# Moving gated-attention decay chains between projections, with a stacked low-rank product and an earlier mask load

## The chip, the cores and the metric

One NeuronCore of a Trainium2 chip runs the whole program. The metric is the time of one execution on the device in microseconds (us), from the profiler's first to last instruction plus what lies around it; several executions are timed and the median is given.

## The reference, cut to what matters

The model is a two-layer backbone on 128 context and 1024 latent tokens (1152 columns in all, width 1024). The even layer projects its normalised input `h` with one matrix into queries, keys and values of a windowed attention (`qa`, `ka`, `va`) and of a gated linear attention (`qb`, `kb`, `vb`, `rb`), and into a low-rank input `lr` of 2 x 16 columns, from which the decay of the gated attention comes:

```python
la = log_sigmoid(einsum('btzr,zrk->btzk', lr, w_alpha) + b_alpha) / 16
bcum = cumsum(la over each chunk of 64 tokens)      # forward, and backward for z = 1
q_e, k_e = q * exp(bcum), k * exp(-bcum)
attn = where(tril mask, q_e k_e^T, 0)
```

Queries and keys of the windowed attention are rotated (`rope_2d`) on latent tokens, and the attention reads all context keys beside its window. The odd layer (a gated recurrence) and the two SwiGLU mixers are not touched by the change.

## The kernel before

The kernel works on transposed activations: features on the 128 partitions, 1152 tokens along the free axis, in three chunks of 384. To keep float32 accuracy, an operand is split into a rounded part `hi` (type float32r) and a rest `lo`, and a product is three matmuls, hi*hi, hi*lo, lo*hi (`mm3`, lines 147 to 150). A projection (`proj`, line 300) is 3 chunks x 8 feature blocks x 3 matmuls = 72 matmuls into a PSUM tile named `mm`; there are three of these (line 105). Small products use tiles named `S`, of which there are two (line 111).

Large buffers are numbered slots of 1152 columns, `us(i)`; each slot has one buffer (`bufs=1`), and a later tile of the same number takes it over. Slots 0 and 1, and 32 and 33, are halves of a double buffer made by `up`. Small staging buffers `tmpa` (name `ta`) exist three times. The program is traced in the order of the text; a planner then orders each engine's instructions by program order and by when it expects operands and buffers to be ready, so work that stands later in the text can run earlier where an earlier piece waits. On each engine the order it has chosen is fixed.

The stages around the change are:

- The normalised input H is made chunk by chunk (`norm`, `norm_k`, lines 263 to 287). Chunk 0 is made ahead; chunks 1 and 2 stand in the block loop at blocks 2 and 5. The input X lies in slots 16 to 23 and is overwritten in place (X[5] is slot 21, X[6] slot 22). A norm sums squares (ACT, DVE), reduces over partitions with small matmuls into an `S` tile (lines 229 and 239, copied at line 260), multiplies on POOL (line 267) and shifts and scales on ACT and DVE (lines 272 to 278), through one `S` tile per feature block.
- The block loop (lines 605 to 623) makes, for each of nine blocks of 128 tokens, the token-major values and the low-rank input in two halves of 24 matmuls each (lines 615 to 617). Line 620 copies a half to a `ta` buffer and line 623 copies the 32 low-rank columns from the second half's PSUM tile to `lrs3`.
- Lines 625 to 639 transpose `lrs3` to `lrt` (32 partitions), build the reset mask RM and load the weights `walp`.
- `gla_pre(hd)` (lines 641 to 655), for each of four heads, is the decay chain: three float32 products (line 647), a bias copy on ACT into slot 31 (line 648), exp and log with a table load each (650, 651), two elementwise steps (649, 652), two scans on DVE (653, 654) and a store of slot 30 to `d_b`. All four heads share slots 30 and 31. All four calls stand ahead of the projections in the text.
- Then come the projections of the attention's keys (w_ef[4]), values (w_ef[5]) and four query pairs (w_ef[0] to [3], lines 677 to 724), with `rope` on DVE and POOL, key stacks on ACT and DVE (`kstack`, lines 711 and 713) and stores to `d_qa`, which `attention` (lines 733 to 832) reads back for all four pairs at once.
- `gla_init` (line 854) stands behind the last attention block; it loads the masks `gmask` through a `ta` buffer. `gla_a` loads the initial states (`sgla`) through another `ta` buffer (lines 904 to 906), and `gla_b` runs the state scans (942, 943).

Of the kernel before, what the change touches and what calls it, by code (L numbers as in the profile page):

```python
# [8 lines left out]
F32R = mybir.dt.float32r  # L9
# [3 lines left out]
ALU = mybir.AluOpType  # L13
# [5 lines left out]
CW = 384  # L19
# [4 lines left out]
U = T  # L24
# [22 lines left out]
def body(tc, A):  # L47
    nc = tc.nc
    ve, sc, pe, gp, sy = nc.vector, nc.scalar, nc.tensor, nc.gpsimd, nc.sync

    def f_(ap):
        return ap.bitcast(F32)

    with contextlib.ExitStack() as ctx:
# [16 lines left out]
        mq = st.tile([128, 2, 128], U8, name="mq")  # L71
        m2 = st.tile([128, 128], F32, name="m2")
# [6 lines left out]
        def up(i, dt=F32):  # L79

            pair[i] = pu.tile([128, 2 * U], dt, tag=f"u{i}", name=f"u{i}", bufs=1)
            return pair[i]

        def us(i, dt=F32):

            if i in (0, 32):
                return up(i, dt)[:, :U]
            if i in (1, 33):
                return pair[i - 1][:, U:]
            return pu.tile([128, U], dt, tag=f"u{i}", name=f"u{i}", bufs=1)  # L90
# [7 lines left out]
        def mmps():  # L98
            if wide[0]:
                wide[0] = wide[0] % 8 + 1  # L100
                if wide[0] > 3 and wide[0] <= wide[1]:
                    return aux(*(("X", 2), ("X", 2), ("S", 2), ("S", 2), ("O", 1))[wide[0] - 4])
                if wide[0] > wide[1]:
                    wide[0] = 1
            return pm.tile([128, 512], F32, name="mm", bufs=3)

        def tmpa(n=CW):
            t = pt.tile([128, CW], F32, name="ta", bufs=3)
            return t[:, :n]

        def aux(tag="S", bufs=2):
            return pm.tile([128, 512], F32, name=tag, bufs=bufs)
# [8 lines left out]
        def wtile():  # L121

            if wext:
                wpos[0] = (wpos[0] + 1) % (4 + len(wext))
                if wpos[0] >= 4:
                    i = wext[wpos[0] - 4]
                    return uc(i - 100, F32R) if i >= 100 else us(i, F32R)[:, :D]
            return pw.tile([128, D], F32R, name="w", bufs=4)
# [3 lines left out]
        def wload(ap, n=D, slots=None, he=None):  # L132
            raw = pw.tile([128, D], F32, name="raw", bufs=3)
            sy.dma_start(out=raw[:, :n], in_=ap)
            if slots:
                hi, lo = us(slots[0], F32R), us(slots[1], F32R)
            else:
                hi, lo = wtile(), wtile()
            (he or wcopy[0])(hi[:, :n], raw[:, :n])  # L139
            gp.tensor_tensor(out=lo[:, :n], in0=raw[:, :n], in1=f_(hi[:, :n]), op=ALU.subtract)  # L140
            return hi, lo

        def split(hi, lo, src, e=None):
            sc.copy(hi, src)
            return (e or ve).tensor_tensor(out=lo, in0=src, in1=f_(hi), op=ALU.subtract)  # L145
# [13 lines left out]
        def ch(c):  # L159
            return slice(c * CW, (c + 1) * CW)  # L160
# [11 lines left out]
        def load_x(c):  # L172
            for k in range(8):
                sy.dma_start(out=X[k][:, ch(c)], in_=A["xT"][k, :, ch(c)])
# [117 lines left out]
        def projc(w, H, evict, c):  # L292
            hi, lo = w
            ps = mmps()
            for k in range(8):
                s = slice(k * 128, (k + 1) * 128)
                mm3(ps[:, :CW], hi[:, s], lo[:, s], H[0][k][:, ch(c)], H[1][k][:, ch(c)], k == 0, k == 7)
            evict(c, ps[:, :CW])

        def proj(w, H, evict):  # L300
            for c in range(NCH):
                projc(w, H, evict, c)
# [259 lines left out]
        d_qa = dr.tile([4, 128, T], F32, name="d_qa")  # L562
# [22 lines left out]
        H = [[None] * 8, [None] * 8]  # L585
# [15 lines left out]
                    sc.copy(wh[:, s], raw)  # L601
                    (gp if hf == 0 or i else ve).tensor_tensor(out=wl[:, s], in0=raw, in1=f_(wh[:, s]), op=ALU.subtract)
        load_x(2)
        lrs3 = us(32)[:, :288].rearrange("p (b n) -> p b n", b=9)
        for blk in range(9):
            if blk in (2, 5):
                norm(0, 0, X, H, 1 if blk == 2 else 2, inplace=True)
# [1 line left out]
            for hf in range(2):  # L609
                ps = mmps()  # L610
# [7 lines left out]
                n = 272 if hf == 0 else 240  # L618
# [3 lines left out]
                if hf == 1:  # L622
                    ve.tensor_copy(lrs3[:, blk], ps[:, 240:272])

        lrt = us(33)[0:32]
        for b0, b1 in ((0, 4), (4, 8), (8, 9)):
            ps = aux()
            n = (b1 - b0) * 128
            for b in range(b0, b1):
                pe.transpose(ps[0:32, (b - b0) * 128:(b - b0 + 1) * 128], lrs3[:, b], ident)  # L630
            ve.tensor_copy(lrt[:, b0 * 128:b1 * 128], ps[0:32, :n])

        RM = us(23)
        gp.memset(RM, 1.0)
        rm = RM.rearrange("p (c t) -> p c t", t=64)
        gp.memset(rm[0:64, :, 0:1], 0.0)
        gp.memset(rm[64:128, :, 63:64], 0.0)
        walp = us(22)[0:32, :512].rearrange("p (h n) -> p h n", h=4)
        sy.dma_start(out=walp, in_=A["w_alp"])

        def gla_pre(hd):

            et, bt = us(31), us(30)
            bal = cols[:, C_BALPHA + hd:C_BALPHA + hd + 1]
            for c in range(NCH):
                ps = aux()
                pe.matmul(ps[:, :CW], walp[:, hd], lrt[:, ch(c)], start=True, stop=True)
                sc.activation(out=et[:, ch(c)], in_=ps[:, :CW], func=AF.Identity, bias=bal)
            ve.scalar_tensor_tensor(bt, et, -1.0, et, op0=ALU.mult, op1=ALU.min)
            sc.activation(out=bt, in_=bt, func=AF.Exp)  # L650
            sc.activation(out=bt, in_=bt, func=AF.Ln, bias=1.0)
            ve.scalar_tensor_tensor(et, et, 0.0, bt, op0=ALU.min, op1=ALU.subtract)
            ve.tensor_tensor_scan(bt[0:64], RM[0:64], et[0:64], 0.0, op0=ALU.mult, op1=ALU.add)
            ve.tensor_tensor_scan(bt[64:128, ::-1], RM[64:128, ::-1], et[64:128, ::-1], 0.0, op0=ALU.mult, op1=ALU.add)
            sy.dma_start(out=d_b[hd], in_=bt)

        for hd in range(4):
            gla_pre(hd)

        COS, SIN = us(16), us(17)  # L660
        sy.dma_start(out=COS[:, :TL], in_=A["rope"][0])
        sy.dma_start(out=SIN[:, :TL], in_=A["rope"][1])
# [1 line left out]
        def rope(t):  # L664
            x = t[:, TC:T]
            r = us(19)[:, :TL]
            ve.stream_shuffle(r, x, [(i + 16) % 32 for i in range(32)])
            ve.tensor_tensor(out=x, in0=x, in1=COS[:, :TL], op=ALU.mult)
            gp.tensor_tensor(out=r, in0=r, in1=SIN[:, :TL], op=ALU.mult)
            ve.tensor_tensor(out=x, in0=x, in1=r, op=ALU.add)  # L670

        def ev_to(t):
            def ev(c, ps):
                sc.copy(t[:, ch(c)], ps)
            return ev

        KA, VST = us(18), us(20)
        proj(wload(A["w_ef"][4]), H, ev_to(KA))
        sy.dma_start(out=A["o_ck"], in_=KA[:, :TC])
        rope(KA)  # L680
        proj(wload(A["w_ef"][5]), H, ev_to(VST))
# [1 line left out]

        KK = [[us(24 + g * 2 + part, F32R) for part in range(2)] for g in range(2)]
        VA = [us(28, F32R), us(29, F32R)]
        SM = us(30, F32R)
        cst = tmpa(256)
        sy.dma_start(out=cst[:, 0:128], in_=A["cache_v"])
        sy.dma_start(out=cst[:, 128:256], in_=A["cache_k"])
        split(SM[:, 0:128], SM[:, 128:256], cst[:, 0:128])  # L690

        def va(part, blk):
            if blk == 9:
                return SM[:, part * 128:part * 128 + 128]
            return VA[part][:, blk * 128:(blk + 1) * 128]

        def kkc(g, part):
            o = 256 + (g * 2 + part) * 128
            return SM[:, o:o + 128]

        for b0, b1 in ((0, 4), (4, 8), (8, 9)):
            ps = aux()
            n = (b1 - b0) * 128
            for b in range(b0, b1):
                pe.transpose(ps[:, (b - b0) * 128:(b - b0 + 1) * 128], VST[:, b * 128:(b + 1) * 128], ident)
            split(VA[0][:, b0 * 128:b1 * 128], VA[1][:, b0 * 128:b1 * 128], ps[:, :n])

# [9 lines left out]
            kstack(cst[:, 128:256], KK[g][0][:, TL:U], KK[g][1][:, TL:U], g)  # L717
            kstack(KA[:, 0:TC], kkc(g, 0), kkc(g, 1), g)

        for j in range(4):  # L720
            q = us(21 + j % 2)
            proj(wload(A["w_ef"][j]), H, ev_to(q))
            rope(q)
            sy.dma_start(out=d_qa[j], in_=q)

# [126 lines left out]
        atr = [0]  # L852

        def gla_init():
            mqf = tmpa(384)
            sy.dma_start(out=mqf, in_=A["gmask"])
            ve.tensor_copy(mq.rearrange("p a b -> p (a b)"), mqf[:, :256])
            ve.tensor_copy(m2, mqf[:, 256:])
            t = us(12)
            gp.memset(t[:, :1024], 0.0)  # L860
            G["AT"] = [t[:, :512], t[:, 512:1024]]
# [144 lines left out]
        for i in range(9):  # L1006
            attention(i - 1)
            if i < 8:
                proj(wload(A["w_ef"][6 + i]), H, ev_spill(d_qk[i], 0.125 if i < 2 else 1.0) if i < 4 else ev_spill(d_r[i - 4], None))
            ada_step(2)  # L1010
            if i == 8:
                gla_init()
                gla_a(0)
# [242 lines left out]
        for blk in range(3):  # L1256
# [3 lines left out]
            g = gates_a(blk, 1)  # L1260
# [172 lines left out]
```

## Time and profile before

| what | value |
|---|---|
| median of 3 runs | 2864.69 us (2863.2 to 2864.82) |
| profiled execution | 2866.14 us, span 2864.4 us |
| PE busy (matmul) | 2671.9 us, 93% of the span |
| DVE, ACT, POOL busy | 71%, 47%, 45% |
| mean granted TensorE clock | 0.96 of full speed |
| chain that ended last | PE 73%, DVE 12%, ACT 5%, DMA 5% |

PE is the TensorE, PEld its weight loads, DVE the VectorE, ACT the ScalarE, POOL the GpSimd, SP the engine that issues most transfers. Busy PE time can hide small gaps, because matmuls overlap. The granted clock says which share of 2.4 GHz the TensorE ran at; 0.50 is the 1.2 GHz level.

### The profile page before, as it was taken

The numbers are of one execution on the slowest core, as the hardware profiler recorded it, in microseconds if no ns is written. First come the engines' busy times: TensorE is split into PE (matmuls) and PEld (weight loads), VectorE is DVE, ScalarE is ACT, GpSimd is POOL, SyncE is SP. The second block draws the span as 40 slices with busy tenths as digits, with TensorE's granted clock in tenths as the row PEclk, the third lists the DMA queues.
The fourth block names the chain that finished last, engine by engine and source line by source line (L and its number), as shares of the span: only waits on it lengthen the run. The fifth ranks groups of instructions, "written<-read, shape, count | busy, mean of one in ns | idle before, by whom it ended". The sixth has DMA issues, their size and how long they took to land.

```text
span 2864.4 us, 48327 instructions
## 1 busy us (share of the span) xinstructions
PE 2671.9 (93%) x18588; PEld 2540.8 (89%) x18588; DVE 2036.7 (71%) x3536; ACT 1333.5 (47%) x2402; POOL 1280.0 (45%) x767
## 2 busy tenths in 40 slices
PE   6999996888899999999999989896899999999998
PEld 4888884556899999999999989896899999999998
DVE  5466677653688877778786566657788777788876
ACT  5445556434543434444335567563543533444333
POOL 4231014223555556455556433333555555455453
PEclk8999997889999999999999999898999999999999
DMA  7125347643342233523223133373342233433322
GB/s 280 58 94 170 127 151 235 198 138 123 109 174 87 84 101 101 202 85 101 82 86 121 61 104 101 110 238 131 129 158 82 89 96 119 162 92 107 101 82 71
DMA packets 136966, 353.64 MB, mean 123 GB/s; under 512 B 14592, under 2 KB 61824, under 8 KB 136736
## 3 DMA queue, kind: packets, MB, share of 16 engines
q1 hardware_dynamic: 135008, 343.48, 36.3%
q0 software_dynamic: 1728, 7.08, 0.7%
q8 instruction: 146, 2.39, 0.3%
q14 instruction: 84, 0.69, 0.1%
HBM read 286.20 MB, written 64.30 MB: 122 GB/s over the span
## 4 chain that ended last, share of the span: by engine, by line
PE 73%; DVE 12%; ACT 5%; DMA 5%; issue 3%; POOL 1%; SPq 0%; DVEq 0%; ACTq 0%; POOLq 0%
PE mm L150 10%; PE mm L148 10%; PE mm L149 10%; PE X L150 5%; PE X L148 5%; PE X L149 5%; PE S L148 4%; PE S L150 4%; PE S L149 4%; PE O L148 2%; PE O L150 2%; PE O L149 2%; PE mm L192 1%; PE X L814 1%; DVE u L943 1%
## 5 line engine op out<-in xcount | busy, mean ns | idle before, releaser
L150 PE MATMUL mm<-u,w 128*128 128x384 f32 (+1 forms) x1320 | 420.9, 321 | 2.4 <-DVE w L458 2.0
L148 PE MATMUL mm<-u,w 128*128 128x288 f32 (+1 forms) x1234 | 396.6, 322 | 25.0 <-DVE u L317 23.1
L149 PE MATMUL mm<-u,w 128*128 128x288 f32 (+1 forms) x1234 | 393.4, 319 | 3.2 <-POOL u L145 3.2
L140 POOL TENSOR_TENSOR w<-raw,w 128x1024 fp32r<-128x1024 f32 (+1 forms) x66 | 150.3, 2278 | 361.3 <-ACT w L139 306.8
L148 PEld LDWEIGHTS mm<-u,w 128*128 128x128 f32 x1234 | 235.5, 191 | 33.8 <-issue 27.9
L150 PEld LDWEIGHTS mm<-u,w 128*128 128x128 f32 x1320 | 251.0, 190 | 7.5 <-issue 4.3
L149 PEld LDWEIGHTS mm<-u,w 128*128 128x128 f32 x1234 | 235.2, 191 | 4.6 <-POOL u L145 3.4
L150 PE MATMUL mm<-u,u 128*128 128x288 f32 x693 | 204.0, 296 | 0.0
L148 PE MATMUL S<-u,w 128*128 128x288 f32 (+1 forms) x526 | 164.9, 314 | 38.9 <-ACT t L1177 33.5
L317 DVE SCALAR_TENSOR_TENSOR u<-mm,mods,u 128x288 f32<-128x288 f32 (+4 forms) x345 | 145.8, 451 | 74.4 <-PE mm L150 73.7
L150 PE MATMUL X<-u,w 128*128 128x288 f32 (+1 forms) x630 | 192.8, 307 | 1.6 <-DVE w L450 1.6
L148 PE MATMUL mm<-u,u 128*128 128x288 f32 x627 | 186.5, 298 | 4.0 <-ACT u L444 3.8
L149 PE MATMUL mm<-u,u 128*128 128x288 f32 x627 | 185.3, 296 | 0.0
L148 PE MATMUL X<-u,w 128*128 128x288 f32 (+1 forms) x580 | 176.2, 306 | 1.4 <-DVE u L145 1.2
L149 PE MATMUL X<-u,w 128*128 128x288 f32 (+1 forms) x580 | 176.3, 305 | 1.1 <-DVE u L278 1.1
L149 PE MATMUL S<-u,w 128*128 128x288 f32 (+1 forms) x526 | 163.5, 311 | 0.0
L148 PE MATMUL mm<-u,c 128*128 128x288 f32 (+2 forms) x497 | 152.4, 307 | 0.7 <-DVE ta L505 0.7
L451 POOL TENSOR_TENSOR u<-raw 128x512 f32<-128x512 f32 x82 | 136.0, 1658 | 35.2 <-DMA raw<-in_w_fi_dram 19.4
L149 PE MATMUL mm<-u,c 128*128 128x288 f32 (+2 forms) x497 | 151.4, 305 | 0.0
L447 DVE TENSOR_TENSOR u<-u,raw 128x512 f32<-128x512 f32 x82 | 140.3, 1711 | 0.8
L148 PEld LDWEIGHTS S<-u,w 128*128 128x128 f32 x526 | 101.7, 193 | 41.8 <-ACT t L1177 35.6
L148 PE MATMUL X<-u,u 128*128 128x288 f32 (+1 forms) x444 | 131.9, 297 | 2.2 <-DVE u L145 1.5
(443 smaller groups left out, 9114.9 us busy)
## 6 DMA issues: line engine op xcount, KB each, us to landing
raw<-in_w_fi_dram SPq DMA_DIRECT2D x164, 512.0 KB, 3.6
raw<-in_w_fo_dram SPq DMA_DIRECT2D x96, 384.0 KB, 3.1
raw<-in_w_ada_dram SPq DMA_DIRECT2D x48, 512.0 KB, 4.9
c<-in_w_ada_dram SPq DMA_DIRECT2D x32, 512.0 KB, 5.9
d_w<-u SPq DMA_DIRECT2D x20, 512.0 KB, 4.0
u<-d_w SPq DMA_DIRECT2D x20, 512.0 KB, 4.8
u<-in_w_ada_dram SPq DMA_DIRECT2D x16, 512.0 KB, 10.3
raw<-in_w_fo_dram SPq DMA_DIRECT2D x16, 512.0 KB, 3.7
```

Source lines behind the costliest of these rows:

```text
L140: gp.tensor_tensor(out=lo[:, :n], in0=raw[:, :n], in1=f_(hi[:, :n]), op=ALU.subtract)
L148: pe.matmul(ps, wh, hh, start=first, stop=False)
L149: pe.matmul(ps, wh, hl, start=False, stop=False)
L150: pe.matmul(ps, wl, hh, start=False, stop=last)
L192: pe.matmul(ps[32 * g:32 * g + 32, :256], scp[:, 4 * p + g], raw[:, g * 256:(g + 1) * 256], start=p == 0, stop=p == 1)
L317: ve.scalar_tensor_tensor(x, ps[:, s0:s1], mod(l, j, cond, n), x, op0=ALU.mult, op1=ALU.add)
L447: ve.tensor_tensor(out=s2, in0=s1, in1=a11, op=ALU.subtract)
L451: gp.tensor_tensor(out=s3, in0=a11, in1=a21, op=ALU.subtract)
L814: pe.transpose(px[:, i * 128:(i + 1) * 128], P[i][:, kb * 128:(kb + 1) * 128], ident)
L943: ve.tensor_tensor_scan(kv[Bk, ::-1], D0[Bk, ::-1], kv[Bk, ::-1], 0.0, op0=ALU.mult, op1=ALU.add)
```

## The change

`lrs3` moves from slot 32 to slot 21. `lrt` becomes a stack of three 32-row groups (hi, hi, lo) in slot 32 and `walp` a stack (hi, lo, hi) in slot 22, so that one matmul over 96 partitions gives hi*hi + hi*lo + lo*hi; the raw weights are loaded to slot 20. The four `gla_pre` calls are put behind the projections of the keys, of queries 0, of queries 1 and of queries 2. Queries 0 and 1 are projected, rotated and stored before the value transposes and the key stacks, in slots 21 and 28; queries 2 keep slot 21 and queries 3 take slot 22. The mask load of `gla_init` moves ahead of the loads of the rotation tables.

```diff
-        lrs3 = us(32)[:, :288].rearrange("p (b n) -> p b n", b=9)
+        lrs3 = us(21)[:, :288].rearrange("p (b n) -> p b n", b=9)
...
-        lrt = us(33)[0:32]
+        lrt = up(32, F32R)[:, :U]
...
-            ve.tensor_copy(lrt[:, b0 * 128:b1 * 128], ps[0:32, :n])
+            g = slice(b0 * 128, b1 * 128)
+            for q in range(2):
+                sc.copy(lrt[q * 32:q * 32 + 32, g], ps[0:32, :n])
+            ve.tensor_tensor(out=lrt[64:96, g], in0=ps[0:32, :n], in1=f_(lrt[0:32, g]), op=ALU.subtract)
...
-        walp = us(22)[0:32, :512].rearrange("p (h n) -> p h n", h=4)
-        sy.dma_start(out=walp, in_=A["w_alp"])
+        walp = us(22, F32R)[:, :512]
+        wa = us(20)[0:32, :512]
+        sy.dma_start(out=wa.rearrange("p (h n) -> p h n", h=4), in_=A["w_alp"])
+        for q in range(2):
+            sc.copy(walp[q * 64:q * 64 + 32], wa)
+        ve.tensor_tensor(out=walp[32:64], in0=wa, in1=f_(walp[0:32]), op=ALU.subtract)
...
-                pe.matmul(ps[:, :CW], walp[:, hd], lrt[:, ch(c)], start=True, stop=True)
+                pe.matmul(ps[:, :CW], walp[0:96, hd * 128:hd * 128 + 128], lrt[0:96, ch(c)], start=True, stop=True)
...
-        for hd in range(4):
-            gla_pre(hd)
-
+        mqf = tmpa(384)
+        sy.dma_start(out=mqf, in_=A["gmask"])
+        ve.tensor_copy(mq.rearrange("p a b -> p (a b)"), mqf[:, :256])
+        ve.tensor_copy(m2, mqf[:, 256:])
...
-        KA, VST = us(18), us(20)
+        KA = us(18)
         proj(wload(A["w_ef"][4]), H, ev_to(KA))
+        gla_pre(0)
+        VST = us(20)
...
+        for j in range(2):
+            q = us(21 if j == 0 else 28)
+            proj(wload(A["w_ef"][j]), H, ev_to(q))
+            gla_pre(j + 1)
+            rope(q)
+            sy.dma_start(out=d_qa[j], in_=q)
+        q2 = us(21)
+        proj(wload(A["w_ef"][2]), H, ev_to(q2))
+        gla_pre(3)
         SM = us(30, F32R)
...
-        for j in range(4):
-            q = us(21 + j % 2)
-            proj(wload(A["w_ef"][j]), H, ev_to(q))
+        for j in range(2, 4):
+            q = q2
+            if j == 3:
+                q = us(22)
+                proj(wload(A["w_ef"][j]), H, ev_to(q))
             rope(q)
             sy.dma_start(out=d_qa[j], in_=q)
...
         def gla_init():
-            mqf = tmpa(384)
-            sy.dma_start(out=mqf, in_=A["gmask"])
-            ve.tensor_copy(mq.rearrange("p a b -> p (a b)"), mqf[:, :256])
-            ve.tensor_copy(m2, mqf[:, 256:])
```

## Rows read from the trace of the kernel before

**Rows 1.** The page's 40 slices (71.6 us each): busy tenths of PE.
```profile
PE   6999996888899999999999989896899999999998
```

**Rows 2.** Waits, 100 to 230 us: total us, times, longest us.
```profile
PE S L647 <- ACT u L648: 8.5, 3, 6.7
```

**Rows 3.** Stages: us, busy PE PEld DVE ACT POOL, granted clock, DMA share, GB/s.
```profile
109.50:131.10 21.60, 20.85 (x100) 16.72 (x99) 9.95 (x6) 9.03 (x11) 4.40 (x1) 1.00 0.01 4
131.10:149.50 18.40, 17.73 (x90) 15.38 (x90) 12.25 (x11) 13.28 (x16) 4.91 (x2) 1.00 0.20 65
149.50:163.00 13.50, 6.80 (x15) 4.25 (x15) 7.44 (x3) 6.31 (x8) 1.12 (x1) 0.62 0.24 84
...
480.00:500.00 20.00, 6.47 (x45) 6.20 (x45) 17.65 (x12) 8.96 (x20) 17.20 (x10) 0.59 0.33 99
```

**Rows 4.** Lines 623, 639 (ns min/median/max, first/last start) and timeline (start, us).
```profile
L623 DVE COPY u<-mm x9: 173/181/181, 56.2 to 105.5; 128x32 f32<-128x32 f32 x9
...
L639 SPq EVENT_SEMAPHORE  x1: 1452/1452/1452, 87.2 to 87.2; - x1
...
87.50 0.68 ACT L275 ACTIVATE S<-u,mods 128x384 f32<-128x384 f32 x1 [0.57 <-DVE u L278]
87.98 0.68 DVE L273 TENSOR_SCALAR S<-u,mods 128x384 f32<-128x384 f32 x1
```

**Rows 5.** Timeline of PE at the end of block 2.
```profile
67.63 0.39 PE L616 MATMUL mm<-u,u 128*128 128x272 f32 x1 [1.06 <-DVE u L278]
```

**Rows 6.** Timeline: norm of chunk 1, then chunk 2.
```profile
53.47 0.50 PE L229 MATMUL S<-ones,t 128*128 128x1 f32 x4
...
56.52 0.48 ACT L260 COPY t<-S 128x384 f32<-128x384 f32 x1
...
66.33 0.78 DVE L254 TENSOR_TENSOR t<-t 128x384 f32<-128x384 f32 x1
...
72.94 0.56 DVE L278 TENSOR_TENSOR u<-S,u 128x384 fp32r<-128x384 f32 x1 [0.85 <-ACT u L277]
...
80.91 7.84 POOL L267 TENSOR_TENSOR u<-u,t 128x384 f32<-128x384 f32 x8 [11.97 <-ACT t L260]
```

**Rows 7.** Timeline of PE behind the longest wait.
```profile
160.52 0.52 PE L149 MATMUL mm<-u,w 128*128 128x384 f32 x1
160.84 0.52 PE L150 MATMUL mm<-u,w 128*128 128x384 f32 x1
...
163.22 0.34 PE L149 MATMUL mm<-u,w 128*128 128x384 f32 x1
163.39 0.33 PE L150 MATMUL mm<-u,w 128*128 128x384 f32 x1
```

**Rows 8.** Timeline of PE at the first low-rank product.
```profile
109.57 0.91 PE L647 MATMUL S<-u,u 32*128 32x384 f32 x2
...
110.41 0.45 PE L148 MATMUL mm<-u,w 128*128 128x384 f32 x1
```

**Rows 9.** Timeline of the chains: ACT and PE.
```profile
116.28 0.58 ACT L648 ACTIVATE u<-S,cols 128x384 f32<-128x384 f32 x1 [1.16 <-PE S L647]
...
131.14 1.05 ACT L648 ACTIVATE u<-S,cols 128x384 f32<-128x384 f32 x2 [6.61 <-DVE u L654]
...
131.77 0.91 PE L647 MATMUL S<-u,u 32*128 32x384 f32 x2 [1.43 <-ACT u L648]
...
156.26 1.65 PE L647 MATMUL S<-u,u 32*128 32x384 f32 x2 [6.70 <-ACT u L648]
...
175.26 1.05 ACT L648 ACTIVATE u<-S,cols 128x384 f32<-128x384 f32 x2 [9.16 <-DVE u L654]
```

**Rows 10.** Line 858, SP's timeline, and the chain that ended last.
```profile
L858 DVE COPY m<-ta x1: 221/221/221, 477.9 to 477.9; 128x128 f32<-128x128 f32 x1
...
471.04 0.46 SPq L856 DMA_DIRECT2D ta<-in_gmask_dram  x1
...
478.90 2.03 issue
```

## The prediction
> **What bounds the kernel now.** I read the page's slices first, then the waits of TensorE, then its busy time by stage. The slices show PE at nine tenths or more nearly everywhere [rows 1], so a microsecond added to or taken from PE's queue is a microsecond of the kernel unless a later stage has slack. The change acts between 45 and 222 us: the nine value blocks (to 105 us) and the stage of projections and decay chains behind them. In the block stage PE is full, with 1.06 us idle [rows 5]. In the next stage it has two kinds of loss. One is a wait: the low-rank matmuls of line 647 wait 8.5 us for line 648, 6.7 us of that in one wait [rows 2]; line 648 in turn waits for the scan of line 654 before it may overwrite its operand [rows 9]. The other is the clock: 149.5 to 163 us ran at a mean grant of 0.62 of full speed [rows 3]. The attention stage behind it, to about 420 us, shows only nines [rows 1], so whatever the change does up to 222 us is passed on. After it, PE has a hole of 13.5 us at 480 to 500 us [rows 3], where head 0 of the gated part starts; the early masks touch that.
>
> **Part 1: `lrs3` moves from slot 32 to slot 21.** This is the largest term and it is a loss. Slot 21 holds X[5] until the third norm (chunk 2), which stands in the program behind the fifth block. Does a new owner of a slot wait for the last reader of the old one, even where the bytes are already free? The kernel before answers: `walp` takes columns 0 to 511 of slot 22 (X[6]), chunk 2 of X[6] is columns 768 to 1151, and SP still waited 1.45 us until 88.65 us, where a last reading of X[6] on DVE ends (87.98 + 0.68 [rows 4]). So it waits. X[5]'s last reader is line 275 at 87.50 us [rows 4], and the first of the nine line-623 copies into `lrs3` ran at 56.2 us [rows 4]. In the new kernel that copy can't run before X[5] is done, and until then its PSUM bank (one of three named mm) isn't free. Blocks 0, 1 and 2 leave one bank each behind; with all three taken PE can't begin block 3. Queued behind it on PE are all later blocks and the key projection; all of these take mm banks, only the norm's small S matmuls still go.
>
> PE ends block 2 at about 66.2 us, where the row with the 1.06 us wait stands [rows 5]. When does X[5] come free? Its sum of squares ends at 66.33 + 0.78 = 67.1 [rows 6]. From the first matmul of a norm's reduction to the copy of line 260 it took 56.52 - 53.47 = 3.05 us for chunk 1 [rows 6]; then 0.48 for the copy, six of the eight multiplies on POOL (7.84 x 6/8 = 5.9 [rows 6]) and 0.68 for line 275 [rows 4]: 10.1 us, so 77.2 us at the earliest. At the latest the reduction gets one of the two S banks only when the second norm is done at 72.94 + 0.56 = 73.5 [rows 6]: then 83.6. I take the middle, 80.4. Wait: 80.4 - 66.2 = 14.2, less the 1.06 that was there: 13.1 us (bounds 10.0 and 16.3). Then the clock: after the 6.70 us wait at 149.5, groups of line 148 to 150 stepped at 0.32 us (160.52 to 160.84) instead of 0.17 (163.22 to 163.39) until about 162.9 [rows 7], 6.6 us at the 1.2 GHz level, so 3.3 us lost. A longer wait should cost the same once. **Part 1: +16.4 us** (10.0 to 19.6).
>
> **Part 2: float32 products become one stacked product.** Each of the 12 products of line 647 is two instructions and holds PE from 109.57 to the next start at 110.41, 0.84 us [rows 8]; a one-pass matmul of the same 384 columns steps by 0.17 [rows 7]. 12 x (0.84 - 0.17) = **-8.0 us**, on PE's own queue. No row shows a stacked product of 96 partitions; I price it as a row of 128, and from below 0 us saved if it needed the old time. The Trainium skill ("FP8 and Floating Point Precision", TensorE Precision Notes) states that a true float32 product takes four passes. By that the old one costs 4 x 0.17 = 0.68 and the saving is 6.1 us; the row's 0.84 decides, so I keep 8.0.
>
> The splits around it (six ACT copies and three DVE subtractions for `lrt`, two and one for `walp`) lie beside the blocks and the key projection, where ACT has 9.0 of 21.6 us busy and DVE 10.0 [rows 3]: nothing. Without that cover the last group alone would be late by about two 0.6 us copies. `walp` is now loaded through a slot (20) that comes free by the same norm; the first low-rank product is behind 12.5 us of projection (72 matmuls x 0.174), so this wait hides too.
>
> **Part 3: the chains are spread.** A chain is line 648, 649, two table loads with Exp and Ln, 652 and two scans. From one head's last bias copy to the next head's first it took 116.28 to 131.14, 14.9 us, for head 0; from product to product or copy 24.5 us (131.77 to 156.26) and 19.0 (to 175.26) for heads 1 and 2 [rows 9]. Before, the four ran one behind the other from 110 us. Now head 0 starts behind the key projection and head 1 only behind two more projections (25 us, against 15 to 19 for the chain), so that wait goes. Heads 2 and 3 each have one projection (12.5 us of PE) before them and a chain of about 19 us: their third product still waits for the scan of the head before, because the two S banks hold the first two. Which PE work the planner puts ahead of it decides how much is idle. Before, it put 17.8 us of PE work (131.77 to 149.56, where the 6.70 us wait begins) against head 1's chain of 24.5. I expect 4 us at each of heads 2 and 3, 8.5 in all as before, but in shorter pieces, without the drop of the clock: the 1.43 us wait at 131.77 [rows 9] left the grant at 1.00 [rows 3]. **-3.3 us**, bounds -11.8 (8.5 and 3.3 both gone) and 0.
>
> **Part 4: masks early.** The mask load (SP, 471.04) took a `ta` buffer ahead of the states of line 905, and a 2.03 us wait at 478.90 in the chain stands before the copies of lines 921 and 928 that go ahead of head 0's scan [rows 10]; the mask's casts end at 478.1 [rows 10]. With that buffer free the wait goes: **-2.0 us**, bounds 0 (the scan waits for the state's landing anyway) and -4. On SP the early mask passes between the block stores; `ta` has three buffers there and the blocks will be waiting for PSUM: nothing. Moving the stores of queries 0 and 1 earlier gains nothing, since attention needs all four.
>
> **Sum.** 16.4 - 8.0 - 3.3 - 2.0 = +3.1 us on the profiled execution's 2866.14 us: 2869.2. The runs' median stands 1.45 below that execution, so 2867.8; I say 2868. A measurement tells about 0.2% (5.7 us, so 2859 to 2870.4) from no change; the forecast is inside.
>
> **Rivals.**
> *The slot isn't held* (1 in 10): the planner gives `lrs3` its place at once. Against it stands the `walp` row. Then part 1 is 0: -13.3, 2851.
> *The wait is at its short end and spreading works fully* (2 in 10): X[5] free at 77.2 and no low clock after the many small norm matmuls (+10.0), no chain waits (-11.8): 10.0 - 8.0 - 11.8 - 2.0 = -11.8, 2853; halfway to it, 2860. For it: 25 us before head 1, and the key stacks (line 711, four casts in the 24.5 us chain) now fall beside head 0. Against: heads 2 and 3.
> *The bank handover* (1 in 4, the other side): the third norm's reduction gets no S bank until the second norm is finished, because each tile of that norm stands ahead of it. Place: between 67.1 and 73.5 us; price: part 1 at 19.6. It decides if X[5] is free after 82 us. With part 3 at its half, 19.6 - 8.0 - 1.6 - 2.0 = +8.0: 2873; with neither part 3 nor part 4, +11.6: 2876.
> *The forecast* (0.45): own range 2863 to 2873.
>
> Chances from these: faster by over 0.2%: the first rival and most of the second, 0.26; slower: the third less its low end, and the top of the forecast, 0.33; the same 0.41. Range 2853 to 2878: it takes the second rival and the third and leaves the first and the far ends out.
>
> **What would show it.** In the new trace: the first copy into `lrs3` behind the last reading of X[5] at 77 to 84 us; a hole in PE from about 66 us, then 6 us at the low clock; the blocks ending at about 120 instead of 105. The low-rank products as 12 single instructions stepping by 0.17. Two shorter waits for the scan, at heads 2 and 3, none at head 1. The scan of head 0 of the gated part about 2 us nearer to its states. If the copies into `lrs3` run while X[5] is still in use, part 1 is wrong and the kernel is faster; if the blocks end at 105 the whole forecast falls.

## The result, and the profile after

The changed kernel takes 2882.06 us (median of 4 runs, 2879.95 to 2884.67); the kernel before, run beside it, 2864.11 us. The ratio is 1.0061 with a 95% interval of 1.0049 to 1.0073. Against the 2864.69 us that the forecast started from, that is 17.4 us slower, where 3.1 us were forecast; the stated range ended at 2878 us. The profiled execution's span is 2879.7 us, 15.3 more than before, at a mean granted clock of 0.96 as before.

The loss is in the block stage. The copies of line 623, which answer to [rows 4] (ns min/median/max, first/last start):

```profile
L623 DVE COPY u<-mm x9: 179/181/181, 84.3 to 123.1; 128x32 f32<-128x32 f32 x9
```

The first copy moved from 56.2 to 84.3 us and the last, the end of the blocks, from 105.5 to 123.1: 17.6 us. The timeline of PE, ACT, POOL and DVE in the changed kernel shows the hole, in place of the 1.06 us of [rows 5]:

```profile
65.14 0.39 PE L615 MATMUL mm<-u,u 128*128 128x272 f32 x1 [2.79 <-ACT ta L620]
...
68.14 0.29 PE L617 MATMUL mm<-u,u 128*128 128x272 f32 x1
72.68 1.44 PE L229 MATMUL S<-ones,t 128*128 128x1 f32 x6 [4.25 <-DVE u L278]
...
84.62 0.57 PE L615 MATMUL mm<-u,u 128*128 128x272 f32 x1 [8.29 <-DVE u L623]
84.99 0.43 PE L616 MATMUL mm<-u,u 128*128 128x272 f32 x1
...
76.92 7.67 POOL L267 TENSOR_TENSOR u<-u,t 128x384 f32<-128x384 f32 x8 [8.19 <-ACT t L260]
...
83.20 0.68 ACT L275 ACTIVATE S<-u,mods 128x384 f32<-128x384 f32 x1 [0.37 <-DVE u L278]
```

Read it downwards. With blocks 0 and 1 each holding a bank, only one is left for the two halves of block 2: the second half waits 2.79 us for the copy of the first (line 620), a wait that the kernel before does not have there. Block 2 ends at 68.4 us. The third norm's reduction (line 229) waits 4.25 us for line 278, the last step of the second norm for a feature block, and begins at 72.68: it got no `S` bank before. POOL multiplies from 76.92, X[5] has its last reader, line 275, at 83.20 + 0.68 = 83.9, and 0.4 us later the first copy into `lrs3` frees the bank for block 3. The windows give the price (us, busy PE, PEld, DVE, ACT, POOL, granted clock, DMA share, GB/s), first after, then before:

```profile
45.00:66.00 21.00, 17.41 (x128) 16.76 (x127) 16.20 (x25) 15.12 (x31) 14.71 (x10) 0.95 0.56 177
66.00:85.00 19.00, 5.90 (x34) 5.33 (x33) 12.70 (x27) 11.16 (x21) 10.41 (x11) 0.63 0.23 72
85.00:105.00 20.00, 20.00 (x150) 20.00 (x150) 3.23 (x10) 3.45 (x7) 1.30 (x3) 0.93 0.10 35
```
```profile
45.00:66.00 21.00, 21.00 (x151) 21.00 (x150) 16.27 (x27) 15.05 (x32) 14.52 (x10) 0.87 0.59 193
66.00:85.00 19.00, 17.94 (x144) 17.72 (x143) 9.84 (x23) 8.88 (x18) 7.03 (x8) 1.00 0.19 60
85.00:105.00 20.00, 20.00 (x162) 19.90 (x161) 6.48 (x16) 5.74 (x11) 5.06 (x7) 1.00 0.29 94
```

PE is busy 43.3 us of these 60 instead of 58.9, 15.6 us less. The low clock behind the hole is short: some 14 matmuls step by 0.23 us instead of 0.13 until 88.0, about 1.5 us.

What should have come back behind the blocks hardly did. From the blocks' end to the first attention matmul it took 116.9 us before (105.5 to 222.4) and 114.9 after (123.1 to 238.0). The stage in windows, after (columns as above):

```profile
160.00:180.00 20.00, 20.00 (x117) 20.00 (x116) 12.92 (x8) 10.02 (x13) 8.36 (x3) 1.00 0.24 91
180.00:198.00 18.00, 15.29 (x88) 14.90 (x86) 11.88 (x9) 8.60 (x11) 5.60 (x2) 1.00 0.27 96
198.00:211.00 13.00, 7.15 (x36) 6.77 (x35) 10.65 (x8) 4.56 (x8) 3.74 (x2) 0.74 0.30 107
...
226.00:238.00 12.00, 6.46 (x39) 5.16 (x40) 5.75 (x10) 3.75 (x10) 2.37 (x1) 0.72 0.71 246
```

PE is full to 180 us, and then has two holes with a low grant, at 198 to 211 and 226 to 238. Where [rows 3] had one hole of that kind (6.80 of 13.50 us, 0.62), there are now two. The rows that end them, the last query's copy on ACT (line 682), and DVE in front of the second hole; the last row is DVE in the kernel before, where the last query's rotation begins:

```profile
136.02 0.51 PE L654 MATMUL S<-u,u 96*128 96x384 f32 x2
136.36 0.34 PE L148 MATMUL mm<-u,w 128*128 128x384 f32 x1
...
184.40 0.44 PE L654 MATMUL S<-u,u 96*128 96x384 f32 x1 [2.71 <-ACT u L655]
...
204.10 0.69 PE L654 MATMUL S<-u,u 96*128 96x384 f32 x1 [5.85 <-ACT u L655]
...
231.54 1.93 PE L192 MATMUL mm<-c,scp 128*32 128x256 f32 x16 [5.55 <-DVE t L865]
...
203.47 1.05 ACT L655 ACTIVATE u<-S,cols 128x384 f32<-128x384 f32 x2 [7.41 <-DVE u L661]
...
215.91 0.49 ACT L682 COPY u<-mm 128x384 f32<-128x384 f32 x1
```
```profile
216.35 4.39 DVE L660 TENSOR_TENSOR_SCAN u<-u,u 64x1152 f32<-64x1152 f32 x1
220.76 2.55 DVE L661 TENSOR_TENSOR_SCAN u<-u,u 64x1152 f32<-64x1152 f32 x1
...
223.56 1.36 DVE L675 STREAM_SHUFFLE u<-u 128x1024 f32<-128x1024 f32 x1
...
229.05 1.23 DVE L678 TENSOR_TENSOR u<-u,u 128x1024 f32<-128x1024 f32 x1
230.92 0.56 DVE L865 TENSOR_SCALAR t<-mm 128x384 f32<-128x384 f32 x1
```
```profile
208.48 0.01 DVE L667 LOAD_MASK_SELECT u<-u  x1 [0.46 <-ACT u L674]
```

The product (now line 654) steps by 0.17 us as priced (two from 136.02 to 136.36). But it waits 2.71 and 5.85 us at heads 2 and 3, together as much as the 8.5 us of [rows 2], because line 655 still waits for the scan of the head before. And the fourth chain's scans stand on DVE in front of the last query's rotation (223.56) and the copy of line 865 (230.92), for which PE waits another 5.55 us. The query that is rotated there was copied by 216.4 (215.91 + 0.49), so its rotation begins 7.2 us late. Before, that rotation began at 208.5, as soon as the copy was done (line 674), with nothing of a chain in front of it.

### The profile page after: what moved, and what is told of

Read it like the earlier page. It is cut to its first block, busy times and chain, and to the rows that moved or that the text cites. A ratio compares the mean times of both kernels' runs of the same rounds, so it can differ in the third digit from the quotient of the medians.

```text
span 2879.7 us, 48327 instructions
## 1 busy us (share of the span) xinstructions
PE 2662.9 (92%) x18576; PEld 2540.2 (88%) x18576; DVE 2026.5 (70%) x3537; ACT 1335.8 (46%) x2409; POOL 1282.8 (45%) x767
## 4 chain that ended last, share of the span: by engine, by line
PE 72%; DVE 12%; ACT 6%; DMA 5%; issue 4%; POOL 1%; SPq 0%; DVEq 0%; ACTq 0%; POOLq 0%
PE mm L150 10%; PE mm L148 10%; PE mm L149 9%; PE X L148 5%; PE X L150 5%; PE X L149 5%; PE S L148 4%; PE S L150 4%; PE S L149 4%; PE O L148 2%; PE O L150 2%; PE O L149 2%; PE mm L192 1%; DMA raw<-in_w_fi_dram 1%; DMA ta<-d_y 1%
```

## The experiments

A ratio is always to the kernel before, run beside it on the same chip; 0.1% is 2.9 us. Milestones of the profiled executions, in us:

| kernel | blocks' end | last scan starts | last query copied | its rotation starts | first attention matmul | ratio |
|---|---|---|---|---|---|---|
| before | 105.5 | 192.5 | 208.4 | 208.5 | 222.4 | 1 |
| changed | 123.1 | 220.8 | 216.4 | 223.6 | 238.0 | 1.0061 |
| before_same | 105.7 | 192.7 | 208.8 | 208.8 | 222.9 | 0.9987 |
| before_hold | 123.9 | 212.6 | 228.7 | 228.7 | 242.7 | 1.0059 |
| after_nohold | 105.8 | 202.8 | 198.4 | 205.6 | 221.2 | 0.9989 |
| before_order | 106.1 | 203.1 | 203.4 | 205.9 | 221.1 | 1.0008 |
| before_stack | 105.7 | 190.7 | 207.2 | 207.3 | 221.1 | 0.9975 |
| before_stack_again | 105.7 | 190.6 | 206.7 | 206.7 | 220.5 | 0.9969 |
| before_mask | 106.1 | 193.1 | 209.2 | 209.3 | 223.3 | 0.9999 |
| before_two | 106.0 | 168.1 | 210.4 | 210.5 | 224.5 | 1.0003 |
| stack_two | 108.8 | 175.3 | 208.9 | 208.9 | 222.8 | 0.9982 |
| before_two26 | 105.7 | 166.3 | 202.0 | 202.1 | 216.1 | 0.9973 |
| stack_two26 | 106.3 | 173.9 | 203.5 | 203.5 | 217.3 | 0.9960 |
| stack_two26_again | 105.0 | 172.7 | 201.8 | 201.8 | 215.7 | 0.9965 |
| nohold_two26 | 105.8 | 203.6 | 199.1 | 206.2 | 222.5 | 0.9997 |
| nohold_early3 | 106.4 | 195.3 | 205.2 | 208.4 | 222.1 | 0.9986 |

The two columns in the middle show who sets the attention's start. In the old order of chains the last query's rotation starts within 0.1 us of the query's copy, and the attention 13.8 to 14.1 us after that copy, in all eleven profiles. In the new order the copy comes as much as 10.0 us earlier (after_nohold, 198.4 for 208.4), but the rotation starts 2.5 to 7.2 us behind it, because other work stands ahead of it on DVE.

**The scale of the noise: before_same.** The kernel before with no edit.

> The kernel before itself once more, as a measure of what two equal programs show, and for a profile on this chip: ratio 1.000 within 0.0015; attention starts at 222 us and the state scans at 483 us, as in the first profile.

2864.4 us, 0.9987 [0.9977, 0.9997]. The interval leaves out 1 for two equal programs, and the low-rank waits were 5.4 us in this profile and 8.5 in the other. So a difference of 0.13% is nothing here, whatever its interval says, and neither are 3 us of waits in one profile.

**The hold alone: before_hold.** The kernel before with `lrs3` in slot 21; `lrt` keeps the columns of slot 33.

```diff
-        lrs3 = us(32)[:, :288].rearrange("p (b n) -> p b n", b=9)
+        lrs3 = us(21)[:, :288].rearrange("p (b n) -> p b n", b=9)
...
-        lrt = us(33)[0:32]
+        lrt = up(32)[0:32, U:]
```

> The kernel before with one thing done: lrs3 in slot 21. Theory A: the first copy into lrs3 runs at about 84 us, the blocks end at about 123 us, and the time is 2864 plus 13 to 18: 2877 to 2882 us. Rival B: the delay is given back by the waits for the scans (8.5 us before) and the time is 2864 to 2870 us.

2881.38 us, 1.0059 [1.0041, 1.0076], which is 16.9 us (11.8 to 21.8). Waits of PE from 40 to 240 us (total, times, longest):

```profile
PE mm L615 <- DVE u L623: 8.3, 1, 8.3
PE S L647 <- ACT u L648: 6.9, 3, 5.1
...
PE S L229 <- DVE u L278: 2.9, 1, 2.9
PE mm L615 <- ACT ta L620: 2.8, 1, 2.8
```

One slot number costs what the whole change costs, with the same waits at lines 615 and 229 (the second one shorter, 2.9 us).

**All but the hold: after_nohold.** The changed kernel with a buffer of its own for the copies (`small` is cut from 128 to 112 columns to make room).

```diff
-        lrs3 = us(21)[:, :288].rearrange("p (b n) -> p b n", b=9)
+        lrs3 = st.tile([128, 288], F32, name="lrs").rearrange("p (b n) -> p b n", b=9)
```

> The changed kernel with one thing undone: lrs3 gets a buffer of its own instead of slot 21. Theory A (the slot held by X[5] is the loss): the three block tiles come free at once, TensorE's hole between 62 and 85 us is gone, the blocks end at 105 instead of 123 us, and 13 to 18 us of the loss go: 2864 to 2869 us. Rival B (the loss is made later, by the new order of chains and queries or by what the planner makes of the stages behind; the early hole would have been absorbed): blocks end at 105 but the time stays above 2875 us.

2863.48 us, 0.9989 [0.9977, 1.0001]: -3.2 us (-6.6 to +0.3), inside what two equal programs show. The blocks end at 105.8 again. The hold is worth 20.6 us here (1.0061 - 0.9989), a little over the 13 to 18 of theory A. From both sides the hold is the loss; and the rest, priced at -13.3 us, is worth little.

**The order alone: before_order.** The kernel before with the new places of the four chains and of queries 0 and 1.

```diff
-        for hd in range(4):
-            gla_pre(hd)
...
         proj(wload(A["w_ef"][4]), H, ev_to(KA))
+        gla_pre(0)
...
+        for j in range(2):
+            q = us(21 if j == 0 else 28)
+            proj(wload(A["w_ef"][j]), H, ev_to(q))
+            gla_pre(j + 1)
...
+        proj(wload(A["w_ef"][2]), H, ev_to(q2))
+        gla_pre(3)
```

> The kernel before with the new order of chains and queries alone (float32 products, lrs3 in slot 32, masks late). Theory C (the four chains follow each other at about 20 us each wherever they stand, and the last query's rotation stands behind the last scan on VectorE, so the chains set the start of the attention; put behind the key projection the first one only starts some 8 us later): attention starts 5 to 10 us later than 222 us and the time is 2868 to 2874 us. Rival D (spreading takes the waits for the scans away, as the forecast had it): 2858 to 2862 us.

2866.9 us, 1.0008 [0.9995, 1.002]: no gain, and between the ranges of both theories. The attention starts at 221.1, not the 5 to 10 us later of theory C. The two largest waits in this stage:

```profile
PE S L647 <- ACT u L648: 5.8, 2, 4.5
PE S L786 <- DVE u L763: 4.7, 1, 4.7
```

The chain waits are down from 8.5 to 5.8 us, within what the equal program showed, and the wait at the attention's start, for the query casts behind the last rotation, is 4.7 us where it was 2.2 before.

**The stacked product alone: before_stack, before_stack_again.** The splits of `lrt` and `walp` as in the change, in the kernel before, with the copies in a buffer of their own.

```diff
-        lrs3 = us(32)[:, :288].rearrange("p (b n) -> p b n", b=9)
+        lrs3 = st.tile([128, 288], F32, name="lrs").rearrange("p (b n) -> p b n", b=9)
...
-                pe.matmul(ps[:, :CW], walp[:, hd], lrt[:, ch(c)], start=True, stop=True)
+                pe.matmul(ps[:, :CW], walp[0:96, hd * 128:hd * 128 + 128], lrt[0:96, ch(c)], start=True, stop=True)
```

> The kernel before with the stacked product alone (lrs3 in a buffer of its own, chains and masks as before). If TensorE's queue bounds the stage (the last query's projection ends at 208 us, 13 us behind the last scan): 8 us less, 2855 to 2858 us. If the chains bound it (theory C holds for the old order too): 0 to 3 us less, 2861 to 2864 us. A second reading: the 12 products step by 0.17 us as single instructions if the price of the forecast was right.

> The stacked product alone once more, beside the others: a second measure of 0.9975 [0.9963, 0.9987]. If the saving of 8 us counted in full it would be 0.9972; if the waits took all of it back, 1.0000. Expected 0.9970 to 0.9985.

0.9975 [0.9963, 0.9987] and 0.9969 [0.9957, 0.9980]: -7.2 and -8.9 us, the second just past the range that was expected. The size is as forecast, within a noise of 3.7 us. But the attention starts at 221.1 and 220.5 us, only 1.3 and 1.9 earlier, and PE waits more for the chains (before_stack):

```profile
PE S L654 <- ACT u L655: 15.9, 3, 9.0
```

So most of the 8 us is not visible as an earlier attention. The chains end where they did, and PE, busy 98.6 us between the blocks' end and the attention in place of 106.2, waits 15.9 us for them in place of 8.5; the last query's copy comes only 1.2 us earlier. Where the rest of the gain appears was not settled. The first state scan is 2.4 and 2.9 us earlier, the end of these two profiles 8.7 and 6.4; but behind the attention single profiles say little, for in before_same, the equal program, the last state scan came 5.7 us later than in the first profile and the end 2.9 us earlier. How much of the -7.2 and -8.9 belongs to the edit is therefore open.

**The early masks alone: before_mask.** The load and the two casts of `gmask` ahead of the rotation tables.

```diff
+        sy.dma_start(out=mqf, in_=A["gmask"])
...
         COS, SIN = us(16), us(17)
```

> The kernel before with the early mask load alone. The forecast's price: 2 us less (0 to 4), the first state scan at about 481 instead of 483 us. Rival: the planner's order behind it shifts, or the scan waits for its states anyway: 0, and a ratio of 1.000.

2866.37 us, 0.9999 [0.9989, 1.0008]: nothing. PE's long wait there (13.5 us at line 962, 440 to 520 us) became one of 12.7 us at line 916:

```profile
PE S L916 <- DVE u L928: 16.0, 3, 12.7
```

The prediction had read the 2.03 us of [rows 10] as a wait for the buffer that the masks held; the view calls it "issue", which names no wait. The copy of line 921 stands behind it. Its row before, and in before_mask:

```profile
480.94 0.27 ACT L921 COPY ta<-S 128x128 f32<-128x128 f32 x1 [2.04 <-issue]
```
```profile
482.17 0.27 ACT L921 COPY ta<-S 128x128 f32<-128x128 f32 x1 [2.04 <-issue]
```

With the masks early the 2.04 us are still there. In both profiles a group of seven matmuls of line 916, which make what this copy reads, ends 0.30 us ahead of it (478.78 + 1.86 before, 480.01 + 1.86 in before_mask), so the copy was waiting for TensorE, as far as these rows tell.

**The chains' waits: before_two, stack_two.** If shared slots 30 and 31 hold the chains apart, a second pair should free them.

```diff
-            et, bt = us(31), us(30)
+            et, bt = (us(31), us(30)) if hd % 2 == 0 else (us(29), us(28))
```

> The kernel before with a second pair of buffers for the decay chains (heads 1 and 3 use slots 29 and 28 in place of 31 and 30), nothing else. Theory C (the chains, one behind the other at 20 us through their two shared slots, set the stage): the bias copies of head h+1 no longer wait for the scans of head h, the four chains end by about 170 instead of 195 us, TensorE's waits for line 648 (8.5 us) and its low clock (3.3 us) go, and the time falls by 8 to 12 us: 0.9958 to 0.9972 of before. Rival E (TensorE's queue bounds the stage, waits are made up for later): within 2 us of before.

> The stacked product (lrs3 in a buffer of its own) and the second pair of buffers together, old order, late masks. In the stacked kernel TensorE waited 15.9 us for the chains, so the 8 us of the product were turned into waiting. Theory C: with the second pair these waits go, attention starts about 16 to 20 us earlier than 221 us, and the time is 16 to 20 us below before: 0.993 to 0.9945. Rival E: no more than the 7 us that the stacked product alone showed.

Theory C missed in both: 1.0003 [0.9995, 1.0012] and 0.9982 [0.9974, 0.9991]. In before_two the chains did end 24 us earlier (last scan at 168.1) and their waits fell to 2.4 us, but the value transposes (line 705) are copied to slots 28 and 29, and now waited for them:

```profile
PE S L705 <- DVE u L145: 6.9, 1, 6.9
...
PE S L647 <- ACT u L648: 2.4, 3, 1.2
```

In stack_two the same wait was 6.9 us, and those for the chains still 7.8.

**A pair that nobody needs soon: before_two26, stack_two26, stack_two26_again.** The same with slots 27 and 26, which the second key stack takes later.

> The kernel before, with nothing changed but the chains of heads 1 and 3 in slots 27 and 26. Theory of the waits: the 8.5 us of chain waits go and no new wait takes their place, so the attention starts at 213 to 217 us instead of 222.4 and the time is 0.9960 to 0.9980 of before. Rival (set off PE): 222 us and 0.9990 to 1.0010.

> The kernel before with the stacked product alone (its copies of the low-rank columns in a buffer of their own), and the chains of heads 1 and 3 in slots 27 and 26, which only the key stack of the second group takes later, in place of 31 and 30. Theory: the 8 us that the stacked product frees on PE come back as waits for the shared slots (15.9 us in the run with the stacked product alone), and the earlier second pair, 29 and 28, only handed the wait on to the value transposes (6.9 us); with 27 and 26 neither is left. Then PE waits under 3 us between the blocks and the attention, the first latent attention matmul starts at 206 to 212 us instead of 222, and the time is 0.992 to 0.9955 of before. Rival: the attention's start is set off PE (query rotations on DVE, loads of the queries): it starts at 220 to 223 us again, at 0.9970 to 0.9985.

> The best version once more, for a second measure of 0.996 [0.9945, 0.9974] (old order of chains, stacked product, chains of heads 1 and 3 in slots 27 and 26). Expected 0.9945 to 0.9970; it beats the kernel before if the interval lies under 0.998.

before_two26: 0.9973 [0.9963, 0.9983], -7.7 us, attention at 216.1, both as the theory had it. Waits 100 to 230 us:

```profile
PE S L647 <- ACT u L648: 2.3, 2, 1.6
PE mm L148 <- ACT u L674: 2.0, 1, 2.0
```

and PE had a granted clock of 0.98 from the blocks' end to the attention, against 0.96 before. With the stacked product on top: 0.9960 [0.9945, 0.9974] and 0.9965 [0.9952, 0.9978], about -11 us: faster than both kernels by more than the noise, though less than the -7.7 and -8.0 of the two alone, and short of the 0.992 to 0.9955 that the theory gave the first. The attention's start, forecast at 206 to 212, came at 217.3 and 215.7: with less PE work the stage ran into waits again (stack_two26).

```profile
PE S L654 <- ACT u L655: 6.3, 3, 3.9
PE S L712 <- DVE u L145: 4.2, 1, 4.2
```

**What sets the attention's start in the new order: nohold_two26, nohold_early3.** The first is after_nohold with slots 27 and 26 for heads 1 and 3. The second also calls the fourth chain behind the third, ahead of the third query:

```diff
             gla_pre(j + 1)
+            if j == 1:
+                gla_pre(3)
...
         proj(wload(A["w_ef"][2]), H, ev_to(q2))
-        gla_pre(3)
```

> The changed kernel without the hold of slot 21 (its copies in a buffer of their own) and with the chains of heads 1 and 3 in slots 27 and 26. Theory: the spread order runs the chains later, so that the last scan and the last query's rotation set the attention's start; with two pairs of slots the chains overlap, the low-rank waits of 8.6 us shrink to under 4 us, the attention starts at 210 to 217 us instead of 221, 0.994 to 0.997 of before. Rival: with the chains spread over the projections, the last chain still stands behind the third query and nothing moves: 0.998 to 1.000.

> The changed kernel without the hold of slot 21, with the chains of heads 1 and 3 in slots 27 and 26, and with the fourth chain called directly behind the third, ahead of the third query's projection instead of behind it. Theory: in the spread order the scans of the fourth chain stand on DVE in front of the last query's rotation (7.0 us in the run with the same slots and the fourth chain behind the third query), and that is what sets the attention's start, not the TensorE. With the chain earlier the last rotation begins within 1 us of the last query's last copy, the first attention matmul comes at 214 to 218 us instead of 222.3, and the time is 0.9955 to 0.9980 of before. Rival: the TensorE's own queue sets it, or the rotation gets behind something else: 221 to 224 us and 0.9985 to 1.0005.

0.9997 [0.9989, 1.0006] and 0.9986 [0.9975, 0.9997]; attention at 222.5 and 222.1: the rival in both. The same pair of slots that gave 7.7 us in the old order gave nothing in the new one. The waits of the two, 100 to 240 us:

```profile
PE S L724 <- ACT u L655: 7.0, 1, 7.0
PE mm L192 <- DVE t L865: 6.0, 1, 6.0
```
```profile
PE S L725 <- ACT u L655: 5.2, 1, 5.2
PE S L798 <- DVE u L775: 4.7, 1, 4.7
PE S L725 <- DVE u L145: 3.4, 1, 3.4
PE mm L192 <- DVE t L866: 0.7, 1, 0.7
```

With the fourth chain earlier, the wait for the copy behind the last rotation falls from 6.0 to 0.7 us, which fits that the scans in front of it caused that one, though the planner has also moved the copy ahead of the rotation's last step. But the value transposes (lines 724 and 725) wait 8.6 us instead of 7.0, the attention's first tiles wait another 4.7, and the theory's price fails: that the scans alone set the attention's start is refuted. In nohold_two26 the last rotation (206.24) does begin right behind the fourth chain's last scan, which ends at 206.2. In nohold_early3 the scans are out of the way, and a row of ACT names what stands there instead:

```profile
201.06 2.10 ACT L731 CAST u<-u 64x1024 fp32r<-64x1024 f32 x2 [8.05 <-DMA d_b<-u]
```

These are the casts of the second key stack into slots 26 and 27, and they wait 8.05 us until the fourth chain's result is stored to `d_b`. The last query's copy stands behind them on ACT and ends at 205.2 us, 6 us later than in nohold_two26; on DVE the key stacks end at 208.35, and the rotation begins at 208.39. In before_two26 the same casts waited 4.7 us, but at 172 us, 30 us ahead of the last rotation. This is read from the rows; no run took that wait away.

## Why the prediction was wrong, step by step

**Part 1, the hold of slot 21: right, at its upper bound.** Place, mechanism and size were forecast: a copy that waits for the last reader of X[5], blocks 0 to 2 leaving a bank each, a hole, a low clock. Of the two cases for X[5]'s release (77.2 or 83.6) the later one came (83.9), so the rival of the bank handover was the true one: its deciding point (X[5] free after 82 us) was met. I took the middle. The hole was 2.5 us longer than the middle gave it (15.6 us of PE for 13.1); the 2.79 us between the halves of block 2, with two of three banks held, were not in the sum. The low clock was 1.8 us cheaper (1.5 for 3.3). 17.6 us at the blocks' end against 16.4; 16.9 us in the time for the hold alone, and 20.6 (1.0061 - 0.9989) inside the change, with an uncertainty of some 5 us.

**Part 2, the stacked product: right in size on PE's queue, wrong in what it brings.** The products were single instructions stepping by 0.17 us, and the edit alone gave -7.2 and -8.9 us. But "on PE's own queue" counts only where PE is what is late. Alone, it brought the attention 1.3 and 1.9 us nearer. In the changed kernel PE was busy 100.8 of 114.9 us between the blocks' end and the attention, 5.4 less than before (106.2 of 116.9), and the stage got 2.0 shorter. The two single measures don't tell the row's 8.0 us from the prediction's other figure, 6.1; both lie in their intervals.

**Part 3, the chains spread: the step that failed.** I wrote that 8.5 us of waits would remain "but in shorter pieces, without the drop of the clock". They remained, 8.6 us at heads 2 and 3 as said, but one piece was 5.85 us, and the clock fell as it had: behind it PE stepped 0.32 us until 207.4, the 1.2 GHz level. And I did not follow the fourth chain to its end: called last, its scans stand on DVE in front of the last query's rotation, which begins 7.2 us after its query is ready (223.6 for 216.4), and PE has a second hole of 5.55 us with a grant of 0.72. So what PE gained stopped at DVE: without the hold (after_nohold) the last query is copied 10.0 us earlier than before, and the attention starts 1.2 us earlier. Measured alone, the order gave +2.3 us (-1.4 to +5.7) for -3.3.

**Part 4, the masks: a gain of 2 us that wasn't there.** -0.3 us alone (-3.2 to +2.3). The 2.03 us were no wait for the masks' buffer: they stood unchanged with the masks early. Head 0's first scan of the states, which was to be 2 us nearer to its loads, is in the changed kernel 15.4 us behind them (479.1 to 494.5) instead of 10.9 (472.0 to 482.9).

**The sum.** The miss is 14.3 us. Some 4.2 of it lie in part 1 (20.6 for 16.4) and 10.1 in the rest (-3.2 for -13.3): nothing in part 2 alone, 5.6 in part 3, 1.7 in part 4, and 2.8 in adding up parts that share one stage. Two of these, 1.7 and 2.8, are below the 3.7 us that equal programs showed, and 5.6 is little above it, so the split is rough. The mechanism is clearer: where only PE's work is cut, the waits grow from 8.5 to 15.9 us. The prediction said whatever the change does up to 222 us is passed on. For the hole it was: +17.6 at the blocks' end, +15.6 at the attention, +15.3 at the end. The mistake was to book the gains in the same way without asking, of each, who is late once it is made. Every case had taken part 2 in full, so the bank handover came out at 2873 to 2876 and not at 2882.

## What to carry to other kernels

A slot whose bytes nothing needs any more was still free only once the last reader of its old owner had run; find that reader's time in the trace and compare it with the first write, before moving a small tile there. A saving on a busy engine counts only until the next chain is late: where work of several engines runs side by side, sum the gains per stage, not per edit, and look for the instruction that is late next. A second buffer is worth what its next owner can wait: slots 28 and 29 handed the wait on to the value transposes, 27 and 26 to the key stacks, which had the time in the old order and not in the new one.

## What the runs showed of the hardware

In the decay chains the same scan of 64 x 1152 takes 2.55 us or, in most other cases, 4.4 to 4.6 us. Line 653 shows both in the kernel before, once beside a POOL instruction:

```profile
148.42 4.61 DVE L653 TENSOR_TENSOR_SCAN u<-u,u 64x1152 f32<-64x1152 f32 x1
...
189.98 2.54 DVE L653 TENSOR_TENSOR_SCAN u<-u,u 64x1152 f32<-64x1152 f32 x1
```
```profile
148.00 2.61 POOL L140 TENSOR_TENSOR w<-raw,w 128x1024 fp32r<-128x1024 f32 x1 [12.07 <-ACT w L139]
```

At 189.98 no POOL instruction was running. In the changed kernel each of the four chains has one slow scan, each beside such a POOL subtraction, as the one at 196.17 (4.63 us) beside 2.62 us at 195.77. The Trainium skill ("SBUF — State Buffer", Who interferes with whom) says that DVE and POOL share a pair of ports under an exclusive lock, so that one of them stands still; the rows agree with it, but no run here took the POOL work away. Such a scan stretches a chain by 2 us, three of the four before and all four after, which the forecast of the chain from [rows 9] holds without saying so.
